# Two-group decoder step: the delta rule's chunk inversions regrouped on three PSUM banks

## The chip, the cores and the metric

One core of a Trainium2 chip runs the whole step. The metric is the device time of one execution in microseconds; smaller is better. The engines are PE (matrix products, with PEld for loading their weights), DVE, ACT and POOL (elementwise work), and SP (which issues DMAs). PE writes to PSUM, in banks of 128 x 512 fp32 values; everything else lies in SBUF.

## The reference, cut to what matters

The program is one step of a hybrid decoder with 2 layers, for a prompt of 512 tokens and a sample group of 8 x 8 tokens that share all weights (model width 1024). In each layer one projection feeds four mixers (sparse attention, a convolution module, retention, a gated delta rule), whose outputs are merged by gates and projected; a gated MLP follows. The change is in the delta rule of 4 heads of 64 channels. For each chunk of tokens:

```python
Lm = exp(where(tri, gc[..., :, None] - gc[..., None, :], -inf))
M = where(strict, einsum('bhncd,bhnsd->bhncs', kb, kc) * Lm, 0.0)
A = M + eye(C)
sol = triangular_solve(A, concat([vc * bc, kb * exp(gc)]), lower=True, unit_diagonal=True)
u, w = split(sol);  att = einsum('bhncd,bhnsd->bhncs', qc, kc) * Lm

def step(S, ...):                      # one chunk after another
    vn = u_ - w_ @ S
    o_ = qd_ @ S + at_ @ vn
    S = S * gl_ + kd_.T @ vn
```

`M`, `att` and the inverse of `A` of a chunk need no other chunk; only `step` goes from chunk to chunk, with the state `S`. The sample group starts from a state per row that is given.

## The kernel before, in words

The prompt is cut into chunks 0 to 3 of 128 tokens; the sample group's 64 tokens are a fifth chunk, number 4. All of the delta rule's core stands in `gdn`, in the phase "gchunk" (from L1031).

`inverse(tt, lane)` (L1039) is a generator for one chunk. It builds decay masks (tiles `LT`, `Ln`; L1053 to L1066), the products k by k and k by q (L1074, L1075), from which come `M` (in `Ln`) and `att` (in `LT`), turns `M` (`U`), and inverts the 128 x 128 triangles of 4 heads by doubling: diagonal blocks of 32 in levels (L1114 to L1135, matmuls of 32 x 32 recorded under L1095), then 64 (`X64`), then 128 (`R64`); the result is `W`. Each level is a batch of 16 small matmuls, a DVE product (`R`, L1121), a batch of 32, and two DVE differences. The fp32 matmuls show two records each in the trace. The function yields 16 times for a prompt chunk, 8 for the sample, each time where the next work waits for another engine. Its PSUM tiles are one bank, named by the lane.

`scan(tt)` (L1174) is the sequential step of a prompt chunk: it reads `att` (L1215) and `W` (L1192, L1198) and updates `S`; 4 or 5 yields. `sample()` (L1236) is the same for the sample's chunk, with its loaded states `S0` (L883), which are masked and reduced on DVE (L899, L901, 128 x 512); 3 yields.

`turns` (L1434) lets the given generators take one step each, in turn; `both` (L1287) counts the turns and after each adds `RATE` to a sum; whenever it reaches 1, `feed` takes a step. `feed` (L1910) issues other work that is ready, for PE above all: half a gate projection or branch product (24 or 6 dense matmuls of 128 x 288 under L346 to L348) with loads and splits of weights (L296 to L299), and fillers (compressed attention blocks, L1514; conditioning weights, L383). It yields 24 times in all.

The order on each engine is not the program's. A planner takes the instructions by priority, which is the order in the program but for some marked ones, simulates costs, and fixes each engine's order ahead of time; an instruction whose inputs it takes to be late lets later ones pass. A tile with a tag has so many slots ("bufs"); a new tile waits until the last reader of the slot's tile before is done, and slots of a tag go round in program order. `LT`, `Ln`, `U`, `W`, `eB` have 2 slots.

Before, the groups of `both` are: the sample's inversion alone; chunk 0's beside `sample()`; chunks 1, 2, 3 each beside the scan of the chunk ahead; the last scan alone. The phase "gout" follows with the z projection (4 halves of 24 dense matmuls).

Of the kernel before, what the change touches and what calls it, by code (L numbers as in the profile page):

```python
# [23 lines left out]
SMP = DB * DS  # L24
# [14 lines left out]
NBUCK = 32  # L39
NOUT_ADA = 6 * D // P  # L40
NMID = 8
RATE = 0.32
LAG = 1
ADA = [[1, 0] * 16, [1, 0] * 16]
GADA = [8, 0]
# [128 lines left out]
class Kern:  # L174
# [45 lines left out]
    def hv(self, name):  # L220
        return self.sp.tile([P, HALF], F32, tag="hv", name=name, bufs=6)
# [714 lines left out]
    def gdn(self, l, par, h, tok, feed):  # L936
# [54 lines left out]
        with self.phase("gconv", True):  # L991
# [6 lines left out]
            for i in range(6):  # L998
                w = self.load_w(self.ap["wtr"][l, M_GQ + i])
                gb = self.pt("ggb", (3 + SEQ + DB * 11,), bufs=2)  # L1000
                gs = gb[:, 3 + SEQ:].rearrange("p (b t) -> p b t", b=DB)
# [29 lines left out]
        with self.phase("gchunk", True):  # L1031
# [4 lines left out]
            hv = lambda t: t.rearrange("p (h t) -> p h t", h=4)  # L1036
            state = {}

            def inverse(tt, lane):  # L1039


                pr = tt < 4
                n, m = (P, 4) if pr else (SMP, 2)
                s = slice(tt * P, tt * P + n)
# [2 lines left out]
                bl = lambda t: t[:, :m, :n]  # L1047
                rows = lambda j: slice(0, P) if pr else slice(j % 2 * 64, j % 2 * 64 + 64)
                un = lambda t, j: t[rows(j), j if pr else j // 2, :n]
                pp = lambda: hv(self.ps(f"x{lane}", 1))  # L1050
                f4 = lambda name: self.pt(name, (4, P), bufs=2)
                GB = pp()
                for j, hd in enumerate(HDJ):  # L1053
                    gcol = col(g, hd) if pr else g[rows(j), 16 + j // 2:17 + j // 2]
                    nc.tensor.matmul(un(GB, j), gcol.to_broadcast([n, n]), tu[rows(j)], start=True, stop=True)
                yield
                LT, Ln = f4("LT"), f4("Ln")
                for j in range(m):
                    c = HDJ[j] if pr else j
                    nc.vector.scalar_tensor_tensor(LT[:, j, :n], GB[:, j, :n], col(gc, c), MU, op0=OP.subtract, op1=OP.add)  # L1060
                    nc.vector.scalar_tensor_tensor(Ln[:, j, :n], GB[:, j, :n], col(gc, c), MP, op0=OP.subtract, op1=OP.add)
                if pr:
                    eB = f4("eB")
                    nc.scalar.activation(eB, GB, AF.Exp)
                nc.scalar.activation(bl(LT), bl(LT), AF.Exp)
                nc.scalar.activation(bl(Ln), bl(Ln), AF.Exp, scale=-1.0)  # L1066
                M, att = Ln, LT
                for e in range(2):
# [8 lines left out]
                    for p in range(w):  # L1077
                        j = w * e + p
# [8 lines left out]
                row = [slice(32 * r, 32 * r + 32) for r in range(4)]  # L1087
                cols = row if pr else row[:2] * 2
                diag = [(j, r) for j in range(m) for r in range(4)]
                f32 = lambda name: self.pt(name, (4, 32), bufs=1 if name == "R" else 2)[:, :m]  # L1090
                p32 = lambda: self.ps(f"x{lane}", 1).rearrange("p (h t) -> p h t", t=32)
                lm = lambda i: lmt[:, i * 32:(i + 1) * 32].unsqueeze(1).to_broadcast([P, m, 32])

                def mm32(out, lhsT, rhs, r, c):
# [1 line left out]
                U, X, W, WT = f4("U"), f32("X"), f32("Wc"), f4("W")  # L1096
# [17 lines left out]
                for lv in range(1, nl):  # L1114
                    end = lv == nl - 1
                    R = f32("R")
# [19 lines left out]
                if pr:  # L1136

                    h0, h1 = slice(0, 64), slice(64, P)
                    X64, R = self.pt("X64", (4, 64)), f32("R")
                    nc.gpsimd.memset(X64[row[0], :, row[1]], 0.0)  # L1140
                    for r in range(2):
                        self.evac(X64[row[r], :, row[r]], X[row[r]])
                    ps = p32()
                    for j in range(4):
                        for r in (0, 2):
                            mm32(ps[row[r + 1], j], U[row[r], j, row[r + 1]], X[row[r], j], r, r + 1)
                    yield
                    for r in (1, 3):
                        nc.vector.tensor_copy(R[row[r]], ps[row[r], :4])
                    ps = p32()  # L1150
                    for j in range(4):
                        for r in (1, 3):
                            mm32(ps[row[r - 1], j], R[row[r], j], WT[row[r], j, row[r]], r, r - 1)
                        mm32(ps[row[1], 4 + j], WT[row[1], j, row[1]], R[row[1], j], 1, 1)
                    yield
                    self.evac(X64[row[1], :, row[0]], ps[row[1], 4:8], -1.0)
                    for r in (1, 3):
                        self.evac(WT[row[r - 1], :, row[r]], ps[row[r - 1], :4], -1.0)

                    R = self.pt("R64", (4, 64))  # L1160
                    p64 = lambda: self.ps(f"x{lane}", 1).rearrange("p (h t) -> p h t", h=8)
                    ps = p64()
                    for j in range(4):
                        nc.tensor.matmul(ps[h1, j], U[h0, j, h1], X64[h0, j], start=True, stop=True)
                    yield
                    self.evac(R[h1], ps[h1, :4])
                    ps = p64()
                    for j in range(4):
                        nc.tensor.matmul(ps[h0, j], R[h1, j], WT[h1, j, h1], start=True, stop=True)
                    yield  # L1170
                    self.evac(WT[h0, :, h1], ps[h0, :4], -1.0)
# [64 lines left out]
            def sample():  # L1236

                att, W = state.pop(4)
                s = slice(SEQ, TOK)
                S0 = self.load_state(l, "stg", ("U", "Ln"))  # L1240
                get = {x: (lambda x=x: self.ps(x, 1)) for x in ("sc", "x0", "ss")}
                sc, x0, ss = (get[x] for x in ("sc", "x0", "ss"))
                ps = sc()
                for p in range(2):
                    r = slice(64 * p, 64 * p + 64)
                    self.turn(ps[r, :P], k[p][:, s], self.ident, p)
                    self.turn(ps[r, 256:256 + P], v[p][:, s], self.ident, p)
                yield
                kbe, kd, vb = (self.pt(x, (256,))[:, :P] for x in ("kbe", "kd", "vb"))
                h2 = lambda t: t.rearrange("p (h d) -> p h d", h=2)  # L1250
                for dst, c, t in ((kbe, 0, be), (kd, 0, kdec), (vb, 256, bh)):
                    nc.vector.tensor_mul(h2(dst), h2(ps[:, c:c + P]), t[:, 16:18].unsqueeze(2).to_broadcast([P, 2, HD]))
                nw = self.pt("nw", (2, P))
                ps = [x0(), ss()]
                for p, e in ((0, 0), (1, 1), (0, 1), (1, 0)):
                    b, c = 64 * e, 64 * p
                    nc.tensor.matmul(ps[p][b:b + 64, :SMP], kbe[c:c + 64, b:b + 64], W[c:c + 64, e, :SMP], start=True, stop=True)
                yield
                for p in range(2):
                    self.evac(nw[:, p, :SMP], ps[p][:, :SMP], -1.0)  # L1260
                out, pw = [sc(), x0()], ss()
                for p, e in ((0, 0), (1, 1), (0, 1), (1, 0)):
                    b, c = 64 * e, 64 * p
                    nc.tensor.matmul(pw[c:c + 64, b:b + 64], W[c:c + 64, e, :SMP], vb[c:c + 64, b:b + 64], start=True, stop=True)
                self.on_state(out, [nw[:, p] for p in range(2)], S0, slice(0, SMP))
                yield
                vn = self.pt("vn", (256,))[:, :P]
                self.own_state(vn, out, [self.ind8[:, :8]] * 2, pw[:, :P])
                ps = ss()
                for e in range(2):  # L1270
                    nc.tensor.matmul(ps[64 * e:64 * e + 64, :16], g[:, 16 + e:17 + e].to_broadcast([P, 64]), self.ind8[:, 8:],
                                     start=True, stop=True)
                glb, mask = small("glb", 16), self.pt("emask", (2, 8))
                nc.scalar.activation(glb, ps[:, :16], AF.Exp)
                for e in range(2):
                    nc.vector.tensor_scalar(mask[:, e], self.ind8[:, :8], eg[:, e:e + 1], None, op0=OP.mult)

                def update(p, t, add):
                    nc.gpsimd.tensor_mul(t, t, glb[:, p * 8:p * 8 + 8].unsqueeze(2).to_broadcast([P, DB, HD]))
                    nc.vector.tensor_add(t, t, add)  # L1280

                self.sample_state(l, S0, "o_gdns", o, att, vn, kd, q, [mask[:, e] for e in range(2)], update,
                                  [sc, x0, ss, ss, x0, sc], ("eB", "eB", "kbe"))
# [3 lines left out]
            def both(*gs):  # L1287
                nonlocal due
                for _ in self.turns(*gs):
                    due += RATE  # L1290
                    while due >= 1:
                        next(feed, None)
                        due -= 1
            both(inverse(4, 0))
            both(inverse(0, 1), sample())
            for tt in range(1, 4):
                both(inverse(tt, (tt + 1) % 2), scan(tt - 1))
            both(scan(3))
            for p in range(2):
                nc.sync.dma_start(self.ap["o_gdnp"][l, p], S[p])  # L1300
# [948 lines left out]
```

## Time and profile before

| | us |
|---|---|
| runs | 2568.92, 2571.22, 2564.43 |
| median | 2568.92 |
| profiled execution | 2563.72 |
| its span | 2561.9 |
| PE busy in the span | 2446.2 |
| DVE busy | 1411.1 |
| ACT busy | 938.0 |
| POOL busy | 613.5 |

PE is the engine that is busy nearly throughout. A busy PE is not a PE at its peak, since matmuls overlap and their ends are modelled; the starts in the timeline tell more. The delta rule's core runs from about 250 to 440 us in layer 0, and from about 1508 to 1710 us in layer 1.

### The profile page before, as it was taken

How to read it: one execution, taken by the hardware profiler on the slowest of the kernel's cores; microseconds unless marked ns; L12 is line 12 of the kernel's file. 1: busy time of each engine (PE TensorE's matmuls, PEld its weight loads, DVE VectorE, ACT ScalarE, POOL GpSimd, SP SyncE). 2: the span in 40 equal slices, each digit the busy share in tenths (PEclk: the TensorE clock that was granted, in tenths of full speed). 3: DMA queues.
4: the chain of work that ended last, by engine and by line, in shares of the span. 5: the costliest groups of instructions: out<-in, count | busy, mean ns of one | idle time of the engine just before them, and what ended most of it. 6: DMA issues, size and time to landing. Idle time of an engine off the chain costs nothing.

```text
span 2561.9 us, 54461 instructions
## 1 busy us (share of the span) xinstructions
PE 2446.2 (95%) x22850; PEld 2178.6 (85%) x22850; DVE 1411.1 (55%) x2918; ACT 938.0 (37%) x1815; POOL 613.5 (24%) x801
## 2 busy tenths in 40 slices
PE   6999999999999999999989999999999999999997
PEld 3769787976789899999977687889677999999997
DVE  5789644445524662534579884443553357444446
ACT  4316222434324543323452342233442355333233
POOL 2102322235522210101122032322635222000012
PEclk8999999999999999999999999999999999999999
DMA  8753355423634132422467433524345233233234
GB/s 313 228 195 120 111 173 196 141 89 113 198 98 156 54 120 87 144 86 83 129 216 243 139 102 128 172 80 130 108 138 172 93 117 123 84 121 109 88 89 128
DMA packets 125637, 346.78 MB, mean 135 GB/s; under 512 B 28652, under 2 KB 48112, under 8 KB 119184
## 3 DMA queue, kind: packets, MB, share of 16 engines
q1 hardware_dynamic: 104592, 275.05, 33.0%
q0 software_dynamic: 20800, 68.25, 8.3%
q8 instruction: 180, 2.95, 0.5%
q14 instruction: 65, 0.53, 0.1%
HBM read 330.77 MB, written 20.73 MB: 137 GB/s over the span
## 4 chain that ended last, share of the span: by engine, by line
PE 78%; DVE 9%; DMA 5%; ACT 3%; issue 3%; POOL 2%; SPq 0%; ACTq 0%; DVEq 0%; POOLq 0%
PE mm L346 20%; PE mm L347 20%; PE mm L348 19%; DMA pg<-cv,ix 2%; PE x L1095 2%; DVE wlo L299 2%; PE adaps L383 1%; PE cmps L1514 1%; DVE cvy L715 1%; DMA raw<-wout 1%; PE mmt L649 1%; PE mmt L647 1%; PE mmt L648 1%; PE t L1634 1%; DMA raw<-wtr 1%
## 5 line engine op out<-in xcount | busy, mean ns | idle before, releaser
L346 PE MATMUL mm<-hh,whi 128*128 128x288 f32 x3136 | 946.1, 302 | 7.3 <-ACT whi L298 4.5
L347 PE MATMUL mm<-hl,whi 128*128 128x288 f32 x3136 | 938.5, 299 | 1.2 <-DVE hl L483 1.1
L348 PE MATMUL mm<-hh,wlo 128*128 128x288 f32 x3136 | 937.5, 299 | 2.1 <-DVE wlo L299 2.1
L299 DVE TENSOR_TENSOR wlo<-raw,whi 128x1024 fp32r<-128x1024 f32 (+1 forms) x320 | 390.5, 1223 | 534.1 <-ACT whi L298 528.9
L346 PEld LDWEIGHTS mm<-hh,whi 128*128 128x128 f32 x3136 | 591.6, 189 | 36.1 <-issue 14.9
L347 PEld LDWEIGHTS mm<-hl,whi 128*128 128x128 f32 x3136 | 595.2, 190 | 15.0 <-issue 9.3
L348 PEld LDWEIGHTS mm<-hh,wlo 128*128 128x128 f32 x3136 | 592.3, 189 | 17.2 <-issue 11.6
L298 ACT ACTIVATE whi<-raw 128x1024 fp32r<-128x1024 f32 (+1 forms) x320 | 334.9, 1048 | 544.3 <-PE mm L347 354.5
L348 PE MATMUL mm<-acth,wlo 128*128 128x288 f32 x704 | 206.5, 295 | 2.1 <-DVE wlo L299 2.1
L347 PE MATMUL mm<-actl,whi 128*128 128x288 f32 x704 | 208.1, 296 | 0.0
L346 PE MATMUL mm<-acth,whi 128*128 128x288 f32 x704 | 208.0, 296 | 0.1
L576 POOL COPY nfp<-gb 128x2 f32<-128x2 f32 x44 | 42.3, 960 | 610.6 <-ACT gb L550 610.6
L1473 POOL DMA_INDIRECT pg<-ck,ix x128 | 131.1, 1024 | 102.9 <-issue 49.4
L1857 POOL TENSOR_TENSOR f<-f,gate 128x288 f32<-128x288 f32 x80 | 72.4, 919 | 291.3 <-DVE gate L1856 290.7
L348 PEld LDWEIGHTS mm<-acth,wlo 128*128 128x128 f32 x704 | 131.9, 188 | 2.9 <-DVE wlo L299 2.6
L347 PEld LDWEIGHTS mm<-actl,whi 128*128 128x128 f32 x704 | 132.9, 189 | 0.9 <-DVE actl L355 0.5
L346 PEld LDWEIGHTS mm<-acth,whi 128*128 128x128 f32 x704 | 132.2, 188 | 1.3 <-ACT acth L354 1.0
L1473 POOL DMA_INDIRECT fil<-cc,ix x64 | 69.2, 1082 | 143.9 <-PE cmps L1514 125.8
L715 DVE SCALAR_TENSOR_TENSOR cvy<-cgb,par,cvy 128x512 f32<-128x512 f32 x120 | 93.4, 791 | 0.0
L1835 ACT ACTIVATE gate<-mm 128x288 f32<-128x288 f32 x112 | 45.3, 404 | 126.0 <-PE mm L348 105.2
L346 PE MATMUL mm<-bh,whi 128*128 128x288 f32 x256 | 80.1, 315 | 1.9 <-ACT ga L1835 1.4
L347 PE MATMUL mm<-bl,whi 128*128 128x288 f32 x256 | 78.5, 307 | 2.3 <-DVE bl L355 2.3
(600 smaller groups left out, 3965.6 us busy)
## 6 DMA issues: line engine op xcount, KB each, us to landing
raw<-wtr SPq DMA_DIRECT2D x124, 512.0 KB
raw<-wup SPq DMA_DIRECT2D x104, 512.0 KB
f<-wada SPq DMA_DIRECT2D x32, 1024.0 KB
fil<-wada SPq DMA_DIRECT2D x16, 1024.0 KB
raw<-wdn SPq DMA_DIRECT2D x32, 512.0 KB
raw<-wdn SPq DMA_DIRECT2D x32, 448.0 KB
raw<-wbr SPq DMA_DIRECT2D x16, 512.0 KB
raw<-wout SPq DMA_DIRECT2D x16, 512.0 KB
```

The source lines that it names most:

```text
L298: nc.scalar.activation(hi, raw, AF.Copy)
L299: nc.vector.tensor_sub(lo, raw, hi.bitcast(F32))
L346: nc.tensor.matmul(ps, hi[:, k0 + k], ah[:, s], start=first, stop=False)
L347: nc.tensor.matmul(ps, hi[:, k0 + k], al[:, s], start=False, stop=False)
L348: nc.tensor.matmul(ps, lo[:, k0 + k], ah[:, s], start=False, stop=last)
L383: nc.tensor.matmul(ps[32 * b:32 * b + 32, :], self.csil[:, k, :], t[:, 512 * b:512 * b + 512], start=k == 0, stop=k == KT - 1, tile_positi ...
L576: nc.gpsimd.tensor_copy(newp[:, ft], g[:, SEQ:SEQ + 2])
L715: nc.vector.scalar_tensor_tensor(y[:, :SEQ], gb[:, j:j + SEQ], wj(j), y[:, :SEQ], op0=OP.mult, op1=OP.add)
L1095: nc.tensor.matmul(out, lhsT, rhs, start=True, stop=True, tile_position=(32 * r, 32 * c))
L1473: self.nc.gpsimd.indirect_dma_start(out=dst, out_offset=None, in_=self.ap[src], in_offset=bass.IndirectOffsetOnAxis(ap=ix[:, l, b, j:j + 1 ...
L1835: self.nc.scalar.activation(gts[hf], ps, AF.Tanh, scale=0.5)
L1857: nc.gpsimd.tensor_add(fm, fm, gm)
```

## The change

Chunks 0, 1 and the sample's are inverted in one group, on the banks x0, x1 and ss; scan 0 follows alone; chunk 2 goes beside `sample()`, and chunk 3 beside scans 1 and 2 in line. `RATE` goes from 0.32 to 0.42. The sample's inversion gets small tiles of its own, of which some lie in the tags `kbe`, `kd` and `vb` of the scans; `X64` moves into the tag `eB` and `R64` into `Ln`; `R` has 2 slots.

```diff
--- before.py
+++ after.py
@@ -39,7 +39,7 @@
 NBUCK = 32
 NOUT_ADA = 6 * D // P
 NMID = 8
-RATE = 0.32
+RATE = 0.42
 LAG = 1
 ADA = [[1, 0] * 16, [1, 0] * 16]
 GADA = [8, 0]
@@ -1047,8 +1047,14 @@
                 bl = lambda t: t[:, :m, :n]
                 rows = lambda j: slice(0, P) if pr else slice(j % 2 * 64, j % 2 * 64 + 64)
                 un = lambda t, j: t[rows(j), j if pr else j // 2, :n]
-                pp = lambda: hv(self.ps(f"x{lane}", 1))
+                pp = lambda: hv(self.ps(lane, 1))
                 f4 = lambda name: self.pt(name, (4, P), bufs=2)
+                if not pr:
+
+                    tags = {"Ln": "kbe", "U": "kd"}
+                    f4 = lambda name: self.pt(name + "s", (2, SMP), tag=tags.get(name))
+                    own = self.pt("vb", (256,))
+                    own = {x: own[:, 64 * i:64 * i + 64].rearrange("p (j t) -> p j t", j=2) for i, x in enumerate(("X", "Wc", "R"))}
                 GB = pp()
                 for j, hd in enumerate(HDJ):
                     gcol = col(g, hd) if pr else g[rows(j), 16 + j // 2:17 + j // 2]
@@ -1087,8 +1093,8 @@
                 row = [slice(32 * r, 32 * r + 32) for r in range(4)]
                 cols = row if pr else row[:2] * 2
                 diag = [(j, r) for j in range(m) for r in range(4)]
-                f32 = lambda name: self.pt(name, (4, 32), bufs=1 if name == "R" else 2)[:, :m]
-                p32 = lambda: self.ps(f"x{lane}", 1).rearrange("p (h t) -> p h t", t=32)
+                f32 = lambda name: self.pt(name, (4, 32), bufs=2) if pr else own[name]
+                p32 = lambda: self.ps(lane, 1).rearrange("p (h t) -> p h t", t=32)
                 lm = lambda i: lmt[:, i * 32:(i + 1) * 32].unsqueeze(1).to_broadcast([P, m, 32])
 
                 def mm32(out, lhsT, rhs, r, c):
@@ -1136,7 +1142,7 @@
                 if pr:
 
                     h0, h1 = slice(0, 64), slice(64, P)
-                    X64, R = self.pt("X64", (4, 64)), f32("R")
+                    X64, R = self.pt("X64", (4, 64), bufs=2, tag="eB"), f32("R")
                     nc.gpsimd.memset(X64[row[0], :, row[1]], 0.0)
                     for r in range(2):
                         self.evac(X64[row[r], :, row[r]], X[row[r]])
@@ -1157,8 +1163,8 @@
                     for r in (1, 3):
                         self.evac(WT[row[r - 1], :, row[r]], ps[row[r - 1], :4], -1.0)
 
-                    R = self.pt("R64", (4, 64))
-                    p64 = lambda: self.ps(f"x{lane}", 1).rearrange("p (h t) -> p h t", h=8)
+                    R = self.pt("R64", (4, 64), bufs=2, tag="Ln")
+                    p64 = lambda: self.ps(lane, 1).rearrange("p (h t) -> p h t", h=8)
                     ps = p64()
                     for j in range(4):
                         nc.tensor.matmul(ps[h1, j], U[h0, j, h1], X64[h0, j], start=True, stop=True)
@@ -1291,10 +1297,14 @@
                     while due >= 1:
                         next(feed, None)
                         due -= 1
-            both(inverse(4, 0))
-            both(inverse(0, 1), sample())
-            for tt in range(1, 4):
-                both(inverse(tt, (tt + 1) % 2), scan(tt - 1))
+            def line(*gs):
+                for x in gs:
+                    yield from x
+
+            both(inverse(0, "x0"), inverse(1, "x1"), inverse(4, "ss"))
+            both(scan(0))
+            both(inverse(2, "x1"), sample())
+            both(inverse(3, "x0"), line(scan(1), scan(2)))
             both(scan(3))
             for p in range(2):
                 nc.sync.dma_start(self.ap["o_gdnp"][l, p], S[p])
```

## Rows read from the trace of the kernel before

**Rows 1.** The page's first lines: span; busy time, share and instructions of an engine.
```profile
span 2561.9 us, 54461 instructions
...
PE 2446.2 (95%) x22850; PEld 2178.6 (85%) x22850; DVE 1411.1 (55%) x2918; ACT 938.0 (37%) x1815; POOL 613.5 (24%) x801
```

**Rows 2.** Windows: stretch, us, busy us (instructions) per engine, granted clock, DMA.
```profile
250.00:440.00 190.00, 187.47 (x3150) 149.03 (x3150) 98.03 (x285) 45.04 (x102) 48.65 (x66) 1.00 0.45 154
460.00:520.00 60.00, 60.00 (x487) 59.06 (x486) 22.11 (x47) 23.75 (x47) 16.39 (x16) 1.00 0.46 140
1508.00:1710.00 202.00, 197.59 (x3233) 162.72 (x3234) 102.58 (x296) 49.97 (x114) 54.85 (x73) 0.99 0.37 122
1593.00:1597.00 4.00, 3.61 (x26) 3.30 (x27) 1.42 (x5) 0.73 (x3) 0.00 (x0) 0.61 0.09 34
```

**Rows 3.** Waits of PE, 250 to 440 us, then 1508 to 1710.
```profile
PE x L1095 <- issue: 1.2, 1, 1.2
PE x L1095 <- DVE R L1121: 0.5, 1, 0.5
PE sc L931 <- DVE oT L901: 0.4, 1, 0.4
PE x L1095 <- DVE X L1135: 0.2, 1, 0.2
...
PE x L1095 <- issue: 2.7, 3, 2.1
PE sc L931 <- DVE oT L901: 0.7, 1, 0.7
PE x L1095 <- DVE R L1121: 0.4, 1, 0.4
PE x L931 <- DVE oT L901: 0.2, 1, 0.2
```

**Rows 4.** Timeline of PE, 283 to 285.5 us: start, us, what.
```profile
283.08 0.29 PE L346 MATMUL mm<-hh,whi 128*128 128x288 f32 x1
283.31 0.45 PE L1095 MATMUL x<-Wc,R 32*32 32x32 f32 x32
283.58 0.48 PE L1095 MATMUL x<-R,Wc 32*32 32x32 f32 x32
283.99 0.40 PE L347 MATMUL mm<-hl,whi 128*128 128x288 f32 x1
284.23 0.30 PE L348 MATMUL mm<-hh,wlo 128*128 128x288 f32 x1
...
284.98 0.45 PE L1095 MATMUL x<-X,U 32*32 32x32 f32 x32
285.36 0.40 PE L347 MATMUL mm<-hl,whi 128*128 128x288 f32 x1
```

**Rows 5.** Timeline of PE, 1590.2 to 1593.5 us; in brackets idle before, releaser.
```profile
1590.84 0.41 PE L1095 MATMUL x<-R,Wc 32*32 32x32 f32 x24
1593.39 0.26 PE L1095 MATMUL x<-R,Wc 32*32 32x32 f32 x8 [2.13 <-issue]
```

**Rows 6.** Lines of DVE, 250 to 282 and 305 to 345 us: busy us, mean ns.
```profile
L1060 DVE SCALAR_TENSOR_TENSOR LT<-x,g_gc,gmA 128x128 f32<-128x128 f32 x4 | 1.4, 341 | 0.0
L899 DVE TENSOR_TENSOR sc<-sc,cst 128x512 f32<-128x512 f32 x1 | 0.7, 700 | 0.2 <-PE x L891 0.2
...
L1111 DVE TENSOR_TENSOR X<-Ln,lm 32x128 f32<-32x128 f32 x4 | 1.2, 292 | 0.0
```

**Rows 7.** DMA queues: packets, MB; whole run, then 1590.9 to 1592 us.
```profile
q8 instruction: 180, 2.95, 0.5%
...
q8 instruction: 1, 0.02, 5.4%
```

**Rows 8.** Timeline of PE, 439.9 to 449 us: the last scan's first and last matmuls.
```profile
439.98 0.33 PE L1181 MATMUL sc<-cst,gqkv 128*128 128x128 f32 x1
...
448.27 0.65 PE L1223 MATMUL sc<-gqkv,gS 64*64 64x128 f32 x8
```

## The prediction

> **What bounds the kernel now.** I read the page's engine sums first: PE is busy for 95% of the span [rows 1]. Then the windows of the two stretches in which the delta rule runs, found by the first and last instruction of its lines: about 250 to 440 us in layer 0 and 1508 to 1710 us in layer 1. PE is busy for 187.47 of 190 us and 197.59 of 202 us there, DVE for about half, ACT for a quarter, at full granted clock [rows 2]. The chains of the delta rule are latency-bound by themselves, but they don't decide the time: the feed's gate and branch matmuls fill every gap. The waits of PE sum to 2.3 us in layer 0 and 4.0 us in layer 1 [rows 3]. The timeline of PE shows the pattern: dense 128x288 matmuls start every 0.13 us, then comes a batch of 32x32 matmuls, then dense ones again; DVE's masking and subtracting between two batches lie beside the dense ones [rows 4]. So a round that falls away gives back its latency to nobody; only stalls, and the friction of changing between dense and small matmuls, are to be had.
>
> **The change, part by part.** *Rounds.* Before, one layer's turns are 9 (sample inversion alone), 17 (chunk 0 beside the sample's state), 3 x 17, and 6 (last scan): 83. After: 17, 5, 17, 17, 6: 62. At 0.32 and 0.42 that is 26.6 and 26.0 feed steps for a feed of 24 yields, which ends at turn 79 of 83 and at turn 60 of 62. The matmuls are the same in number and shape, so with PE full the 21 turns fewer cost and save nothing: 0 us. If the cover were gone, a turn would be worth its round, about 1.7 us (283.31 to 284.98) [rows 4].
>
> *Friction.* Where a small batch stands alone, the dense matmul ahead lasts 0.23 instead of 0.13 us (283.08 to 283.31) and the first one after it 0.24 (283.99 to 284.23): 0.21 us for the pair. A batch of 32 records costs 0.27 us when another follows (283.31 to 283.58) and 0.38 alone (284.98 to 285.36): 0.11 more [rows 4]. So each joining of two batches saves 0.32 us. Turns in which a second or third chain is active: before 4 (sample) + 5 + 6 + 6 = 21; after 17 + 9 in the first block, 4, and 11: 41. Of these 20 more, five are not real (inversion 3 and scan 1, below): 15. How many become neighbours on PE is the planner's doing, since it slips dense matmuls between batches whose inputs come some tenths apart. Before, layer 0 has some 122 small groups (64 + 8 of the inversions, 7 of the sample, 19 of scans, 24 fillers) in gaps between 79 dense stretches, which I counted in the timeline: a third already have a neighbour. I take 0.4: 15 x 0.4 x 0.32 x 2 layers = 3.8 us saved. Ends: all 20 join, 12.8 us saved; a few groups less than before join, +3 us.
>
> *Stalls.* The 6.3 us of waits, and 1.6 us lost where the clock was granted at 0.61 for 4 us (between the levels of 1.2 and 2.4 GHz, right after PE had stood for 2.13 us) [rows 2, 3, 5]: 7.9 us at most. The sample's output products waiting for DVE's reduction are 1.3 us of it; that work moves to a place where DVE is freer, and I count 1.0 as gone. The waits for R and X (1.1) should halve where a second lane fills: 0.5. The 3.9 us "issue" I leave. Together 1.5 us saved; ends 7.9 saved and the first rival below.
>
> *DVE in the first block.* Chunk 1's set-up comes in: 8 for LT and Ln, 4 for M and 2 for att at about 0.34, 10 for X and W at 0.29: 7.7 us. The sample's masks, reductions and updates go out: 10 at 0.70 [rows 6]: 7.0 us. DVE had been near full until 250 us, so the set-up is late by this 0.7 us, beside dense matmuls: 0, with ends of -1 and +1.
>
> *Shared buffers and queues.* The two loads of the sample's state (256 KB each, SP's queue) now take slots that chunk 0's U and R64 leave, so they are issued at the end of the first block. Queued behind them on SP are weight loads; their split has been waiting for a buffer that PE frees, so there is slack, and the state is wanted only after scan 0 and two turns: 0, with an end of +2. X64 on eB's slots waits for POOL's products of q, R64 for M's last reader, the sample's small tiles give theirs to scan 0: all of these ended many turns before: 0, with an end of +1 each.
>
> *Inversion 3.* LT and W have two slots. Chunk 1's are held until scan 1 has read them, and chunk 3 wants just these, in the same block. So it can only multiply its first masks until scan 1 is through; one scan takes 8.9 us (439.98 to 448.92) [rows 8]. What hides it is dense work: while the feed still has steps, PE takes those; behind it the four z-projection halves, 24 x 0.13 = 3.2 us each, of which three fit in PSUM: 9.6 us. I take 0; the other end is 8.9 us per layer.
>
> **Sum.** -3.8 - 1.5 = -5.3 us. The profiled execution took 2563.72 us (1.8 outside the span), so its like would take 2558.4; it lies 5.2 below the median of the three runs, and the forecast goes by the median: 2568.9 - 5.3 = **2563.6**, own range 2559 to 2568.
>
> **Rivals.**
>
> *Slower: PE's instructions come late.* Both long "issue" waits lie inside a run of 32x32 matmuls (2.13 us at 1591.26, the other 1.2) [rows 3, 5], and the instruction queue moved a packet within that stall's window [rows 7]. The page has 180 such packets for 45,700 matmul and load records: 254 each [rows 1, 7]. Chunks 0, 1 and the sample side by side issue 928 records of these small matmuls and as many loads within 17 turns, 7.3 packets, where before one chunk had 424. A late packet costs 1.2 to 2.1 us, with a slow clock behind it 3.7. From two more per layer on the sign turns (2 x 1.7 x 2 = 6.8 against 5.3); with 3.5 per layer and one slow stretch in each, 2 x (6.0 + 1.6) = 15.2 comes on: 2579. Against it: with PE full, the dense matmuls stretch the block, and three such waits long enough to see in eight inversions is few. Chance 0.12.
> The Trainium skill, Runtime: NRT & Kernel Launch, section "Instruction fetch mechanics", says that crossing a block of instructions is mostly hidden; by it this rival would cost 0. The row of 2.13 us with no releaser doesn't agree.
>
> *Slower: inversion 3 runs bare.* Its last turns come 8.9 us late with the feed used up: 17.8 us for both layers, less 5.3: 2581. Decides if the planner has drawn the dense work forward during scan 1. For it: the slots leave no choice; against it: the z-projection. In this sense the change doesn't do what it says, since chunk 3 stands beside one scan, not two. Chance 0.09.
>
> *Faster: the lanes really close up.* All 20 joinings and most stalls: -12.8 to -20.7, central -15: 2554. For it: three equal lanes step alike; against it: their DVE work is serial. Chance 0.23.
>
> *Nothing.* The planner mixes as before and one stall replaces another: 2569. Chance 0.14.
>
> *Faster by far: the stage isn't full.* If what limits it were the chains after all, 21 turns of 2.3 us (190 over 83) in each layer would go: 2472. Against it: 6.3 us of waits. Chance 0.02.
> The Trainium skill, Perfetto Trace Analysis, section "Identifying the Most-Contended Engine", holds that matmul busy time misleads and weight-load busy time tells how full PE is. By it the stage is at 78% (149.03 of 190) where the dense stretch after it is at 98% [rows 2], and filling it would save 190 x (1 - 0.784/0.984) = 39 us a layer. I read the difference as short loads of 0.1 us under small matmuls, which the change keeps.
>
> **How the numbers follow.** Forecast 0.40, the lanes 0.23, nothing 0.14, instructions 0.12, inversion 3 0.09, far faster 0.02. One can't tell less than 0.3%, or 7.7 us, from no change. The forecast's own spread puts a quarter of it past -7.7: faster 0.10 + 0.23 + 0.02 = 0.35; same 0.30 + 0.14 + 0.03 = 0.47; slower 0.18. The range of 8 in 10 goes from 2550 to 2580 and leaves out the far case, a little of the close lanes and the upper halves of the two slower cases.
>
> **What would show it.** Right: PE still at 98% and more in both stretches; fewer dense stretches (about 70 for 79 a layer) and longer runs of small matmuls at their start; no wait of L931 for oT. Wrong: waits "issue" above 4 us a layer in the first block; a stretch near the end where dense matmuls are missing and DVE's LT of chunk 3 waits for scan 1's products; or a stage shorter by tens of us.

## The result: slower by 1.2%, and the profile after

The changed kernel takes 2596.72 us (median of 4 runs, 2594.12 to 2599.76), the kernel before 2567.02 in the same comparison: a ratio of 1.0121, with an interval of 1.0098 to 1.0144. That is 33 us above the forecast, on the other side of no change, and outside the range.

The first lines of the page (span; busy time, share and instructions of an engine), for [rows 1]:

```profile
span 2595.0 us, 54440 instructions
...
PE 2452.6 (95%) x22850; PEld 2190.2 (84%) x22850; DVE 1410.0 (54%) x2918; ACT 937.4 (36%) x1815; POOL 614.1 (24%) x801
```

By this line nothing has happened: as many matmuls, PE at 95%. The span is 33.1 us longer. I set marks at the same two instructions of both traces, the store of the output `o_gcs` ahead of the delta rule and that of `o_gdnp` behind it. Layer 0's stretch is 204.9 us long before and 223.1 after, layer 1's 200.0 and 210.1. So 28.3 of the 33.1 us arise in the two stretches; the rest (2.3 ahead of the first, 2.8 between them, -0.3 behind) is no more than these parts differ by from kernel to kernel below. Windows of the kernel after (columns as in [rows 2]): the two stretches, and the 28 us in each where the first group's small matmuls run.

```profile
246.80:469.90 223.10, 205.59 (x3281) 166.25 (x3279) 106.23 (x302) 50.31 (x114) 53.39 (x79) 0.92 0.41 142
...
1526.20:1736.30 210.10, 195.07 (x3223) 163.53 (x3222) 105.73 (x302) 49.91 (x114) 56.33 (x81) 0.94 0.35 117
...
270.00:298.00 28.00, 15.98 (x858) 14.36 (x858) 15.45 (x64) 0.27 (x1) 0.00 (x0) 0.53 0.06 21
1549.00:1577.00 28.00, 16.10 (x861) 14.21 (x861) 15.96 (x67) 0.28 (x1) 0.00 (x0) 0.61 0.08 22
```

The same of the kernel before: its two stretches, and the 36 and 34 us from the first small matmul on.

```profile
244.50:449.40 204.90, 202.37 (x3284) 160.45 (x3283) 107.87 (x303) 50.62 (x114) 52.73 (x79) 1.00 0.46 159
1502.90:1702.90 200.00, 195.59 (x3224) 160.29 (x3223) 106.76 (x302) 50.52 (x114) 56.24 (x81) 0.99 0.37 123
...
259.00:295.00 36.00, 34.36 (x664) 23.52 (x663) 24.06 (x66) 6.36 (x15) 10.41 (x15) 1.00 0.30 104
1517.00:1551.00 34.00, 32.98 (x645) 24.51 (x646) 23.37 (x67) 6.38 (x15) 6.57 (x11) 1.00 0.15 48
```

PE stands idle for 17.5 of 223.1 us, where it was 2.5 of 204.9 (the difference of the first two columns), and for 15.0 of 210.1 against 4.4 of 200.0. So idle time explains 15.0 of the 18.2 us in layer 0 and all of the 10.1 in layer 1. Most of it lies in the first group: 12.0 and 11.9 us of those 28, at a granted clock of 0.53 and 0.61.

What is missing there shows when the same windows are asked for the tile `mm`, the PSUM tile of the dense 128x288 matmuls (PE, PEld, DVE, ACT; clock; DMA). After, then before:

```profile
270.00:298.00 28.00, 2.05 (x7) 1.64 (x7) 1.26 (x3) 0.00 (x0) 0.53 0.06 21
1549.00:1577.00 28.00, 2.21 (x7) 1.62 (x8) 1.26 (x3) 0.00 (x0) 0.61 0.08 22
```

```profile
259.00:295.00 36.00, 17.54 (x95) 13.02 (x94) 1.72 (x4) 1.21 (x3) 1.00 0.30 104
1517.00:1551.00 34.00, 19.44 (x106) 14.86 (x107) 1.71 (x4) 1.20 (x3) 1.00 0.15 48
```

Seven dense matmuls in place of about a hundred, and beside them some 850 records of small matmuls where the longer windows of before have some 460. I read the order so: with three chains side by side nearly always one has a batch whose inputs the planner takes to be there, and it lets dense work in only where none has; the last experiment bears this out, but no run looks into the planner. The feed's matmuls stand ahead of the first batch and behind the group.

What PE then waits for, in layer 0's stretch and in layer 1's, for [rows 3]:

```profile
PE x L1101 <- issue: 6.6, 5, 1.6
PE sc L931 <- POOL vx L925: 2.9, 1, 2.9
PE x L1101 <- DVE X L1118: 2.8, 2, 2.3
PE ss L1101 <- DVE vb L1118: 1.8, 1, 1.8
PE mm L346 <- issue: 1.6, 1, 1.6
PE mm L347 <- issue: 0.6, 1, 0.6
PE x L1101 <- DVE R L1127: 0.5, 1, 0.5
...
PE x L1101 <- issue: 7.2, 5, 2.1
PE x L1101 <- DVE X L1118: 2.8, 2, 2.3
PE sc L931 <- POOL vx L925: 2.0, 1, 2.0
PE ss L1101 <- DVE vb L1118: 1.8, 1, 1.8
PE x L1101 <- DVE R L1127: 0.5, 1, 0.5
```

In layer 0 the waits with no releaser ("issue") are 7.6 us more than before, DVE's masks and differences 4.4 more, the sample's product for POOL 2.5 more: 14.5 of the 15.0 us. In layer 1 these are 4.7, 4.7 and 1.1, of 10.6. The timeline of PE where the three chains run, for [rows 4] and [rows 5]:

```profile
278.69 0.76 PE L1101 MATMUL x<-X,U 32*32 32x32 f32 x34
280.94 0.59 PE L1101 MATMUL x<-X,U 32*32 32x32 f32 x27 [1.50 <-issue]
...
282.42 0.45 PE L1101 MATMUL x<-Wc,R 32*32 32x32 f32 x16
284.49 0.38 PE L1101 MATMUL x<-Wc,R 32*32 32x32 f32 x12 [1.62 <-issue]
...
301.93 0.44 PE L347 MATMUL mm<-hl,whi 128*128 128x288 f32 x1
302.17 0.44 PE L348 MATMUL mm<-hh,wlo 128*128 128x288 f32 x1
...
304.40 0.29 PE L347 MATMUL mm<-hl,whi 128*128 128x288 f32 x1
304.54 0.29 PE L348 MATMUL mm<-hh,wlo 128*128 128x288 f32 x1
```

A run of matmuls of one kind (34 records, then 27) is cut in two by 1.50 us; 1.62 us cut the run behind 282.42 in the same way. The lower rows show the price of the clock: it was granted at 1.2 GHz from 271.8 to 302.6 us, and the dense matmuls that come behind the group still start every 0.24 us, until 0.13 is back.

PE's instructions come in packets of 16 KB. The whole run has 180 of them for 45,700 matmul and load records and 399 records of semaphore instructions on PE's queue, so a packet is 256 records; the 254 of the prediction left the semaphores out. Counted with them, the five long "issue" waits of layer 0's first group have these numbers of records ahead of them:

| end, us | 280.94 | 284.49 | 288.27 | 292.27 | 296.81 |
|---|---|---|---|---|---|
| idle, us | 1.50 | 1.62 | 1.58 | 1.03 | 1.61 |
| records ahead | 4034 | 4289 | 4545 | 4801 | 5057 |
| the packet of the instruction queue before it starts at | 278.16 | 282.17 | 285.75 | 289.83 | 294.20 |

They stand 255 or 256 records apart, one packet each, and each ends 2.3 to 2.8 us after a packet starts. Between two of them PE works for 1.9 to 3.0 us (284.49 less the idle 1.62 is 282.87, 1.93 after 280.94); from end to end a block lasts 3.6 to 4.5. The instruction queue in this stretch of the kernel after (272 to 298 us), and in that of before (259 to 295), for [rows 7]:

```profile
q8 instruction: 7, 0.11, 1.9%
```

```profile
q8 instruction: 4, 0.07, 0.7%
```

### The profile page after: what moved, and what is told of

It reads as the page before. It is cut to its first block, busy times and chain, and to the rows that moved or that the text cites. A ratio compares the mean times of both kernels' runs of the same rounds, so it can differ in the third digit from the quotient of the medians.

```text
span 2595.0 us, 54440 instructions
## 1 busy us (share of the span) xinstructions
PE 2452.6 (95%) x22850; PEld 2190.2 (84%) x22850; DVE 1410.0 (54%) x2918; ACT 937.4 (36%) x1815; POOL 614.1 (24%) x801
## 4 chain that ended last, share of the span: by engine, by line
PE 77%; DVE 8%; DMA 5%; ACT 4%; issue 4%; POOL 2%; SPq 0%; POOLq 0%; ACTq 0%; DVEq 0%
PE mm L346 20%; PE mm L347 19%; PE mm L348 19%; PE x L1101 2%; DVE wlo L299 2%; DMA pg<-cv,ix 1%; PE adaps L383 1%; ACT whi L298 1%; PE mmt L649 1%; PE mmt L648 1%; PE mmt L647 1%; PE cmps L1524 1%; DMA raw<-wout 1%; DMA raw<-wtr 1%; PE o L1651 1%
## 5 line engine op out<-in xcount | busy, mean ns | idle before, releaser
L1483 POOL DMA_INDIRECT pg<-cv,ix x64 | 71.1, 1111 | 39.6 <-PE o L1812 21.1
```

Source lines behind the costliest of these rows:

```text
L1483: self.nc.gpsimd.indirect_dma_start(out=dst, out_offset=None, in_=self.ap[src], in_offset=bass.IndirectOffsetOnAxis(ap=ix[:, l, b, j:j + 1 ...
```

## The experiments

Theory A: in the first group PE is left with small matmuls alone, since the dense ones are planned around it; it uses its instructions up faster than they come, meets DVE's masks uncovered, and loses the clock. Rivals: the other PSUM and SBUF slots (C), the state loads on SP's queue (B in the first four runs), and later, each as B of its own run, the feed's rate, the third lane, and a wait of certain matmuls that the trace doesn't show. Idle time of PE, of which with no releaser, and clock are those of the two stretches between the marks, in us; where the feed is drawn later, part of the dense work lies behind the mark (some 220 to 250 matmuls a layer in e5_rate). The last column is the longest run of small matmul records with no other matmul between them, in each layer. The code shown is the lines that matter; in these kernels `both` takes a `rate`.

| kernel | ratio to before | idle in the two stretches | of it issue | clock there | longest bare run |
|---|---|---|---|---|---|
| before | | 2.5, 4.4 | 1.2, 2.7 | 1.00, 0.99 | 64, 64 |
| changed | 1.0121 (1.0098 to 1.0144) | 17.5, 15.0 | 8.8, 7.4 | 0.92, 0.94 | 528, 528 |
| e1_dense | 1.0053 (1.0036 to 1.0070) | 7.9, 7.5 | 4.7, 4.0 | 0.98, 0.95 | 160, 160 |
| e2_poolq | 1.0109 (1.0090 to 1.0129) | 15.4, 14.4 | 8.7, 6.5 | 0.92, 0.94 | 528, 528 |
| e3_plumb | 1.0012 (0.9996 to 1.0027) | 2.1, 4.9 | 0.7, 3.3 | 1.00, 0.98 | 64, 64 |
| e4_split | 1.0018 (1.0006 to 1.0030) | 3.0, 7.4 | 0.5, 5.1 | 1.00, 0.99 | 96, 96 |
| e5_two | 1.0061 (1.0044 to 1.0077) | 6.3, 6.6 | 5.0, 4.0 | 0.98, 0.97 | 160, 192 |
| e5_feed07 | 1.0102 (1.0085 to 1.0119) | 12.2, 9.4 | 6.1, 4.1 | 0.95, 0.96 | 384, 384 |
| e5_rate | 1.0157 (1.0140 to 1.0174) | 14.8, 11.7 | 9.4, 6.0 | 0.89, 0.94 | 528, 528 |
| e5_shift | 1.0153 (one run) | 15.2, 15.0 | 8.3, 7.2 | 0.92, 0.92 | 592, 592 |
| e6_dummy | 1.0169 (1.0141 to 1.0197) | 6.1, 8.4 | 0.7, 3.7 | 0.95, 0.96 | 80, 80 |
| e6_bare | 1.0000 (0.9987 to 1.0013) | 1.8, 3.2 | 0.0, 1.7 | 1.00, 1.00 | 64, 64 |

**More feed in the first group.**

```
-RATE = 0.42
+RATE = 0.19
-            both(inverse(0, "x0"), inverse(1, "x1"), inverse(4, "ss"))
+            both(inverse(0, "x0"), inverse(1, "x1"), inverse(4, "ss"), rate=1.0)
```

> The changed kernel with one thing other: in the first group (chunks 0, 1 and the sample) the feed gets 1.0 step per turn instead of 0.42, in the later ones 0.19, so that the feed's total stays. In the order fixed for PE, the first 400 small 32x32 matmuls of a layer then have some 190 dense 128x288 ones between them, where the changed kernel has 6. Theory A (the dense work between the small matmuls is missing, so PE stands for DVE's masks and for its own instructions, and the clock falls): most of the 30 us come back, 2562 to 2578, and waits 'issue' of PE in 240 to 300 us fall from 8.8 us to under 3. Theory B (SP's queue holds the weight loads behind the load of the sample's state, 38.6 us in the changed kernel): that wait stays, the feed can't run ahead, and the time stays above 2588.

2577.97 us against 2563.43: A's range holds it, at its edge, but not "most" of the loss is gone; it is about half, and with it 17 of the 25.6 us of added idle time. The waits "issue" from 240 to 300 us fell to 1.4 us. The three lanes and their slots are as in the changed kernel, so neither costs the half that went. The first group is nearly cured:

```profile
265.00:300.00 35.00, 32.74 (x739) 27.22 (x738) 20.56 (x72) 5.07 (x9) 9.23 (x8) 1.00 0.43 143
```

2.3 us idle in 35 us, at full clock. What remains lies later, where the feed is now thin: slow clock from 376 to 380 and 390 to 397 us, for 21.8 us in layer 1.

**The state loads on another queue.**

```
-                S0 = self.load_state(l, "stg", ("U", "Ln"))
+                S0 = self.load_state(l, "stg", ("U", "Ln"), nc.gpsimd)
```

> The changed kernel, with the two loads of the sample's state issued from POOL's queue instead of SP's, so that no weight load stands behind them. Theory A: no gain, 2593 to 2601, and still almost no dense matmul between the first group's small ones. Theory B: the weights come early, and 15 us or more come back: below 2582.

2590.80 us against 2563.43: 2 us below A's range, but the interval of the ratio overlaps that of the changed kernel, and idle time and clock are nearly the same. In the changed kernel the load stands on SP from 268.8 to 307.49 us, and the next weight loads go out at 312.78. With the load on the other queue they still go out only at 309.87, since SP's next one waits 43.9 us for DVE's `wlo`. So the state load isn't what holds the weights; a few us at most hang on it.

**The changed slots with the groups of before.**

```
-RATE = 0.42
+RATE = 0.32
-            both(inverse(0, "x0"), inverse(1, "x1"), inverse(4, "ss"))
-            both(scan(0))
-            both(inverse(2, "x1"), sample())
-            both(inverse(3, "x0"), line(scan(1), scan(2)))
+            both(inverse(4, "x0"))
+            both(inverse(0, "x1"), sample())
+            for tt in range(1, 4):
+                both(inverse(tt, f"x{(tt + 1) % 2}"), scan(tt - 1))
```

> The changed kernel's tiles, tags and banks with the groups and the rate of the kernel before (0.32; the sample's inversion alone, chunk 0 beside the sample's state, chunks 1 to 3 each beside a scan). Theories A and B: as the kernel before, 2563 to 2571, since the groups are what costs. Theory C (the shared slots of X64, R64 and the sample's small tiles make the stall): 2580 or more.

2566.26 us against 2563.43. Every shared slot, tag and small tile of the change is in it, and it can't be told from the kernel before. C is out.

**The first group taken apart.** Chunk 0 beside the sample's inversion, chunk 1 beside scan 0; the last three groups as changed.

```
-RATE = 0.42
+RATE = 0.35
-            both(inverse(0, "x0"), inverse(1, "x1"), inverse(4, "ss"))
-            both(scan(0))
+            both(inverse(0, "x0"), inverse(4, "ss"))
+            both(inverse(1, "x1"), scan(0))
```

> The changed kernel with the first group taken apart: chunk 0 beside the sample's inversion, then chunk 1 beside scan 0; the rest as changed; 74 turns at 0.35. The order fixed for PE has some 140 dense matmuls among the first 400 small ones, but 13 among the first 200. Theory A: a part comes back, 2570 to 2584, with a shorter stall in the first group. Theory B: the load of the state waits only for chunk 0, so most of it comes back: 2563 to 2572.

2567.72 us: 1.0018, so nearly all of the loss is gone, though chunk 3 still stands beside two scans and chunk 2 beside the sample's state. The loss is made in the first group. By the ranges B came true here and A missed, which wanted 2570 or more; B itself is out by e2_poolq. The working of A counted the feed's matmuls alone, 13 among the first 200 small ones. In the trace fillers (L1524) and the set-up of chunk 1 (L1061, L1187) stand between the batches as well, so that no more than 96 small records follow each other; the clock is full, and one "issue" wait of 0.54 us is left in layer 0. (The profile is of the slowest of its 10 runs, 2578.18 us.)

**Instructions moved against their blocks.** The first products of chunk 0 are issued three times.

```
-                    for j, r in diag:
+                    for j, r in diag * (3 if tt == 0 and lv == 1 else 1):
```

> The changed kernel in which the first 16 small products of chunk 0 are issued three times over into the same places: 32 matmuls and 32 weight loads more at the start of each layer's first group, nothing else changed (time for some 64 records more, about 1 us a layer). In the changed kernel the waits of PE with no releaser that last over 0.4 us end at the 4034th, 4289th, 4545th, 4801st and 5057th record (matmuls and weight loads counted from the start), all at 193 or 194 modulo 256. Theory A (PE runs out of instructions, which come in blocks of 256): they stay at 193 or 194 modulo 256, and so fall on matmuls that stand 64 records earlier in the program of the changed kernel; five of them again, 2595 to 2600 us. Rival B (each of them is a wait of a certain matmul for something that the trace doesn't show): they move with their matmuls to 1 or 2 modulo 256.

One run, 2601.53 us. The long waits have 4034, 4289, 4546, 4801, 5057 and 5313 records ahead of them in layer 0 and 27329, 27585, 27841, 28097 and 28353 in layer 1: all 193 or 194 modulo 256. The expectation had counted 64 records more; the trace shows 64 matmuls and 64 loads, 128 records, more in layer 0, so B wanted 65 or 66 there, not 1 or 2. In layer 1 it is 256 records, a whole block, so that layer 1 can't tell the two apart. (The planner also moved the lanes against each other a little.) Layer 0 decides against B, and so do the other traces: the 71 waits "issue" of over 0.5 us in the two stretches of all 12 kernels stand at 193 or 194, whatever matmul they fall on. So these waits belong to the place in the stream of instructions, not to a matmul, and PE is out of instructions there. The time lies 4.8 us above the changed kernel's median and just over the range that A gave, with six such waits for five; a single run against medians of another comparison says no more.

**The rate alone.**

```
-RATE = 0.42
+RATE = 0.32
```

> The changed kernel with the feed drawn at 0.32 a turn, as before, in place of 0.42. Theory A (what costs is that PE has no dense matmuls among those of the three lanes in the first group; how fast the feed is drawn doesn't bring them there): the same order in the first group, 2594 to 2603 us. Rival B (0.42 uses the dense work up too early): 2564 to 2575 us.

2605.26 us: the rate of before makes it worse, by more than A had said. The first group stays bare (14 dense matmuls in 28 us, at 1.2 GHz throughout):

```profile
275.00:303.00 28.00, 4.39 (x14) 3.63 (x15) 1.25 (x3) 0.00 (x0) 0.50 0.01 4
```

Why it is 8 us worse than the changed kernel stays open. PE's idle time over the whole run is not longer (139.5 us against 142.4), but its mean granted clock is lower (0.973 against 0.977); in layer 0 the slow clock goes on to 318.9 us.

**Two lanes.** The sample's inversion first, then chunks 0 and 1 side by side.

```
-RATE = 0.42
+RATE = 0.36
-            both(inverse(0, "x0"), inverse(1, "x1"), inverse(4, "ss"))
+            both(inverse(4, "ss"))
+            both(inverse(0, "x0"), inverse(1, "x1"))
```

> The changed kernel with its first group taken in two: the sample chunk's inversion alone, then chunks 0 and 1 side by side, at 0.36 a turn; the groups after it as changed. Two lanes now run beside each other where there were three, but the feed's matmuls still don't stand among theirs for long (41 among the last 320 of the 32x32 matmuls of the two, after 66 beside the sample's). Theory A (it is the missing dense work, whatever the lanes): 2573 to 2592 us, with a stretch of slow granted clock and waits of PE for instructions and masks in the two lanes' group, up to 10 us a layer. Rival B (it takes the third lane: three chains' masks one after the other on DVE): 2562 to 2571 us, waits as before.

2578.74 us, within A's range: two prompt chunks side by side are enough for half of the loss. (Chunk 0 beside the sample's shorter inversion, in e4_split, was not.) Waits "issue" are the most of the idle time in both layers, and all but one of the six long ones (1.42 and 2.18 us in layer 0; 1.66, 0.89 and 1.23 in layer 1) stand in the group of the two chunks, at 193 or 194 modulo 256 again.

**A middle dose.**

```
-RATE = 0.42
+RATE = 0.3
-            both(inverse(0, "x0"), inverse(1, "x1"), inverse(4, "ss"))
+            both(inverse(0, "x0"), inverse(1, "x1"), inverse(4, "ss"), rate=0.7)
```

> The changed kernel with the feed drawn at 0.7 a turn in the first group and 0.3 after it: 84 dense matmuls stand among the first 400 of the 32x32 matmuls, where the changed kernel has 6 and the one with 1.0 and 0.19 has 192. Theory A (the loss goes with the stretch in which PE has small matmuls alone): between those two, 2580 to 2593 us, the first 200 small matmuls still bare and slow. Rival B (the dense work only has to be somewhere in the group): 2572 to 2579 us, as with 1.0. Rival C (the loss isn't in the missing dense work): 2593 to 2602 us.

2589.34 us, between the changed kernel and the dose of 1.0. The dense matmuls come among the second half of the small ones only; three of the five long waits of layer 0's first group are left (1.45, 1.87 and 0.89 us).

**Dense work of no use in the gaps.**

```
+                def dummy(ps):
+                    for _ in range(6 if tt < 2 else 0):
+                        nc.tensor.matmul(ps[:, 8:], h[0][0][:, :P], h[0][0][:, :256].rearrange("p (h t) -> p h t", t=32), start=True, stop=True)
...
                         mm32(ps[row[r], j], U[row[r], j, cols[r]], X[row[r], j], r, r)
+                    dummy(ps)
                     yield
...
                             mm32(ps[row[r], 4 + j], W[row[r], j], R[row[r], j], r, r)
+                    dummy(ps)
                     yield
```

> The changed kernel with 6 dense matmuls (128x256, on finished inputs, into columns that nothing reads) behind each of the 16 batches of chunks 0 and 1 in the first group: 96 a layer, 192 in all, work that is of no use. At 0.12 us each at full clock this is 23 us of PE time more. Theory A (in the first group PE stands idle for instructions and masks, some 15 us a layer, and at half clock, because nothing dense stands there): the matmuls go into the idle time; the waits with no releaser fall from about 8 us a layer to under 4, the granted clock is mostly full, and the whole takes 2588 to 2604 us, no more than some us above the changed kernel. Rival B (PE is full there, and the loss is something else): the 23 us come on top: 2615 to 2625 us.

2606.45 us: between the two, 2 us over A's range and 9 below B's. The windows of layer 0's stretch and of its first group, and the waits of PE in that stretch:

```profile
248.40:471.70 223.30, 217.20 (x3376) 176.75 (x3375) 106.43 (x302) 50.47 (x114) 53.29 (x76) 0.95 0.41 142
270.00:300.00 30.00, 27.20 (x865) 23.49 (x865) 16.64 (x68) 0.88 (x2) 0.00 (x0) 0.88 0.08 22
```

```profile
PE sc L931 <- POOL vx L925: 2.2, 1, 2.2
PE ss L1101 <- DVE vb L1122: 1.1, 1, 1.1
PE x L1101 <- DVE X L1122: 0.8, 2, 0.5
PE x L1101 <- issue: 0.7, 1, 0.7
```

Layer 0's stretch holds 96 dense matmuls more and is as long as without them (223.3 against 223.1): they went into the idle time, and the waits for instructions fell from 8.8 to 0.7 us. In layer 1 they fell from 7.4 to 3.7, and its stretch grew by 7.8 us. So the gaps are real room for dense work, more fully in layer 0 than in layer 1, though the clock is still slow for 20.5 and 17.1 us.

**A single chain with less feed.** The kernel before, with no feed steps drawn in its first two groups.

```
-            both(inverse(4, 0))
-            both(inverse(0, 1), sample())
+            both(inverse(4, 0), rate=0.0)
+            both(inverse(0, 1), sample(), rate=0.0)
```

(0.42 a turn for the other groups.)

> The kernel before (one inversion at a time, its own tiles) with no feed steps drawn in its first two groups and 0.42 a turn after them: 106 dense matmuls among the first 400 of the 32x32 matmuls, where the kernel before has 232. Theory A in its wide form (missing dense work costs, whatever the grouping): PE waits for DVE's masks between the batches of the single chain, waits in layer 0's stretch from 2.5 us up to 8 to 20 us, but waits with no releaser stay under 3 us, since a single chain uses its instructions up slowly; 2575 to 2605 us. Rival B (it takes the side by side lanes): 2562 to 2572 us.

2564.05 us against 2564.09: A in its wide form is wrong. The planner brought 94 dense matmuls into 256 to 300 us even so, from work that other groups issue:

```profile
256.00:300.00 44.00, 17.99 (x94) 13.30 (x95) 1.38 (x4) 1.21 (x3) 1.00 0.21 66
```

So with a single chain the feed's steps are not what decides. While it waits for DVE, PE is free in the plan and dense work comes in from wherever it is; with two prompt chunks or three lanes the plan has no such gap unless the feed is drawn faster, as in e1_dense. This narrows A: the lanes side by side make the group bare. It also says that a count of dense matmuls doesn't rank the kernels: among the first 400 small matmuls of layer 0's planned order stand 106 here and 107 in the kernel of two lanes, which loses 0.6%.

The longest bare run ranks them better (last column of the table): 64 records before and in the two kernels that can't be told from it, 96 where 0.2% is lost, 160 to 192 where 0.5% and 0.6% are lost, 384 at 1.0%, 528 and more at 1.1% to 1.6%. e6_dummy has 80 and few waits, but its added work costs time of its own. No run changes this length alone.

## Why the prediction was wrong

*Rounds* is the step that failed: "with PE full the 21 turns fewer cost and save nothing: 0 us". PE was full over the whole stretch of [rows 2] because each chain left gaps and dense work filled them. The change takes just those gaps out of the first group, and the dense work with them: 7 dense matmuls where there were about 100. So the sentence carried a property of the old order over to the new one. The condition of its fallback, the cover gone, came true, but not its price: by it each of the 21 turns fewer would have saved 1.7 us, and the runs show 15.0 and 10.6 us more of idle time in the two layers instead. That taking this group apart gives nearly all back (e4_split), while slots (e3_plumb) and queue (e2_poolq) don't, shows the place.

*Rival "PE's instructions come late"* had the mechanism, the place and nearly the block (254 records for 256); e5_shift shows it. It got 0.12 because "with PE full, the dense matmuls stretch the block": the same step again. It was priced at 3.5 waits a layer and one slow stretch; there were five in each first group, and DVE's masks and POOL's product came uncovered as well, 6.9 us more in layer 0 and 5.8 in layer 1. The Trainium skill, Runtime: NRT & Kernel Launch, section "Instruction fetch mechanics", has such a crossing mostly hidden; here that holds where dense matmuls stand between the small ones (one long wait in each stretch of the kernel before, of some 25 crossings), and not where 256 records are used up in 1.9 to 3.0 us: there the crossings show 1.0 to 1.6 us in layer 0.

*Friction.* Batches did join: [rows 4] has dense matmuls again after 64 small ones, now 111 small ones follow each other. If the slow clock is priced by rows, 35 dense ones at 0.11 us and 816 small ones at 0.16 per 32 (those 111 take the 1.48 us from 280.94 to 282.42, 0.43 per 32, against 0.27) cost 7.9 us in layer 0; what idle time leaves unexplained there is 3.2. By this estimate 4.7 us were saved there, against 1.9 forecast for a layer; no run isolates it.

*Stalls.* The wait of L931 for `oT` is gone, as foreseen (0.4 and 0.9 us), and another stands in its place: 2.9 and 2.0 us for POOL's `vx`. In layer 0 `vx` stands on POOL right behind a product that had waited 5.4 us for a filler's DMA. e4_split keeps the same place for the sample and has no such wait in layer 0 (1.0 us in layer 1), so the place alone doesn't make it.

*DVE in the first block.* Balanced over the block the forecast had 0.7 us; but the set-up of three chains now stands ahead of the first batch, and the sample's masks went out behind it. The first small matmul comes 23.6 us after the mark (270.4 us), before 15.0, and then PE waits 2.3 us for `X` and 1.8 for `vb`. The forecast summed the work over the block and didn't ask when in it.

*Shared buffers and queues*: 0 with an end of 2 fits e3_plumb, which can't be told from the kernel before, and e2_poolq, which moves the time by no more than its interval. *Inversion 3*: 0 was right; PE shows no wait for scan 1 in the last groups.

*Faster by far* is excluded: the kernel with 21 turns fewer is slower. The rule of the Trainium skill on weight-load busy time (Perfetto Trace Analysis, section "Identifying the Most-Contended Engine"), which went with it, would have shown the loss no better: that share fell from 78% to 75% of the stretch, for matmul busy time from 99% to 92%.

Of the signs that were named, two came against the forecast: waits "issue" above 4 us a layer in the first block, and PE below 98% in both stretches (92% and 93%). Of the signs for it, the wait of L931 for `oT` is gone, for the reason given under *Stalls*.

No version here beats the kernel before: e6_bare and e3_plumb can't be told from it.

## What to carry to other kernels

"The engine is full" belongs to an order, not to a stage: before counting a round as free, look at what the new order leaves beside it, group by group, and above all whether independent chains side by side will crowd out the long instructions that covered them. A long run of very short instructions has a price of its own, the delivery of instructions; look in the planned order for the longest run with no long matmul in it, and keep long matmuls among the short ones. And of work that moves within a block, ask when in the block it falls, and not only how much it is.

## What the runs showed of the hardware

In layer 0 of the changed kernel, runs of 32x32 matmuls with at most four dense ones among 256 records work those records off in 1.9 to 3.0 us, while a block of them follows the last one only after 3.6 to 4.5; in the stretches of all these traces the 71 waits "issue" of over 0.5 us stand at 193 or 194 records modulo 256, matmuls, loads and semaphores of PE's queue counted, those at 4546 and 29122 in the kernel before included. PE issued 858 matmuls in 28 us, 57% busy by the trace, and was granted 1.2 GHz nearly throughout; full clock came back at 302.6 us, when dense matmuls had followed each other since 297.92. With dense matmuls of no use between the batches, the waits for instructions of layer 0 went from 8.8 to 0.7 us, and its stretch was as long as without them.
